# Three column tiles of a decoder layer's input projection computed side by side instead of one after the other

## The chip, the cores and the metric

The kernel runs on one core of one Trainium2 chip. The metric is device microseconds (us) of one execution, the median of several runs. TensorE (PE) multiplies, ScalarE (ACT), VectorE (DVE) and GpSimd (POOL) do the elementwise work, and SyncE (SP) issues every DMA from one queue, in the order of the program.

## The reference

One step of one decoder layer for 512 prompt tokens and 32 sample tokens (8 sequences with 4 new tokens each), all in float32:

```python
h = rms_norm(x, norm_pre)                    # over the 2048 model channels
z = jnp.einsum('btd,de->bte', h, w_in)       # 2048 x 7680: q, k, v, gates, conv inputs
att = attend(q, k, v)                        # 12 heads, three dilated windows; samples read a cache
u = c_a * jax.nn.sigmoid(c_b)                # conv branch: depthwise conv, LayerNorm, swish, pointwise
mix = jnp.concatenate([att * silu(g_att), c * silu(g_conv)], axis=-1)
y = jnp.einsum('bte,ed->btd', mix, w_out)    # 2048 x 2048
return x + rms_norm(y, norm_post), new_conv, new_kv
```

The updated cache (`new_kv`) is an output too: most of its bytes are a plain copy of the old cache.

## The kernel before

All 544 tokens lie along the free axis, and channels lie on the 128 partitions. x comes transposed, in 16 blocks of 128 channels (eight loads `xr0` to `xr7` of two blocks each, six buffers). The input projection has 60 column tiles of 128 columns, the output projection 16. The weights of a tile come in four quarters (`raw`, 128x512, 256 KB, six buffers); quarter m belongs to tile m // 4.

Products keep float32 accuracy by splitting both operands in two reduced-precision parts: x into `xh` (ACT, line 243) and `xl` (DVE, line 244), a weight quarter into `wh` (ACT, line 793) and `wl` (POOL, line 794). For each of the 16 blocks of rows and each half of the tokens (272) there are three matmuls: xh by wh, xl by wh, xh by wl. A tile is thus 16 x 2 x 3 = 96 matmuls, which accumulate in two PSUM banks, one for each half.

`split_x(c)` splits the two blocks of one x load. It also sums the squares of x for the RMS norm: ACT squares most blocks (`sq`, three buffers), DVE each fourth (line 250), and the sums of even blocks are added by POOL and those of odd blocks by DVE (`ssum`, line 254). The norm is a factor R for each token, applied when a product is taken out of PSUM by DVE (`evac`, or lines 879 to 882 for queries). `make_R` calls `token_rsqrt`: TensorE sums the squares over the partitions (`rqx`), ACT and DVE form the inverse root, DVE builds five diagonal matrices (line 201), TensorE spreads them over all partitions (`rbx`), and ACT copies them to R (line 295).

`project(n)` computes tile n. For the first tile it alternates: split two loads of x, split the next weight quarter, multiply. The first tile's product is taken out after `make_R`; the tiles behind it find all of x split. `split` looks two quarters ahead (`LOOK`) and loads five further (`AHEAD`). After each quarter comes `tick()`: it advances the side work (attention, conv, samples, the bias tables of `make_tabs`) by a step, and tops up the bulk copy:

```python
        bulk(START + PACE * pe[0])
```

`bulk` issues copies of old cache rows (1152 KB each) on SP's queue as long as the bytes sent stay below a budget: START bytes, and PACE bytes for each row passed through TensorE so far (`pe[0]`). So the DMA traffic that no one waits for is spread over the kernel. Each engine executes its instructions in the order in which the program gives them; `in_order` fixes that.

`make_tabs` is side work added after the first tile: two small products `tb` (line 279) with a copy by ACT each (line 280), then a memset and a small DVE product `lt` (lines 283, 284), and two products `rb` (line 289) with a copy by ACT each (line 290). All four use PSUM bank "s". From the fourth tile on, the samples' cache rows are loaded in units (`kvf`, `kvm`) and DVE computes their scores.

Of the kernel before, what the change touches and what calls it, by code (L numbers as in the profile page):

```python
# [18 lines left out]
P = 128  # L19
# [21 lines left out]

# ticks (quarters of a weight tile) for a batch's keys and for its values
UTK, UTV = 3.8, 3.7
# bytes in the DMA queue: at the start, and for each row that passes through the tensor engine
START, PACE = 8_000_000, 158.35

# [4 lines left out]
def backward(t, c0, c1):  # L51
    # columns c0..c1 of a 512-column tile, the last one first, counted from the end
    a = t[:, 0:1]
    return bass.AP(tensor=a.tensor, offset=a.offset + SEQ - 1 - c0, ap=[list(a.ap[0]), [-1, c1 - c0]])
# [28 lines left out]
def body(tc, xT, w_in, w_out, ckv, cconv, relb, vecs, pww, c_oht, c_ohr, c_lmr, c_tm, c_pick,  # L83
# [12 lines left out]

    # rows that the products given so far pass through the tensor engine
    pe = [0]
# [26 lines left out]

# [1 line left out]
    raws = {}  # L127
# [17 lines left out]
    def load_w(m):  # L145
        # a quarter of a tile: four of its 16 blocks of rows
        if m >= 4 * NTILE or m in raws:
            return
        n, qt = divmod(m, 4)
        raw = wpool.tile([P, 4, P], F32, tag="raw", name=f"raw{m}", bufs=6)  # L150
        dma(raw, w_in[order[n], qt] if n < N_IN else w_out[n - N_IN, KORD[4 * qt] // 4])
        raws[m] = raw
# [3 lines left out]

# [1 line left out]
    ident = keep.tile([P, P], F32, name="ident")  # L158
# [7 lines left out]
    dtab = dram.tile([NH, TW], F32, name="dtab")  # L166
    # rows 32g + 4h + t: biases of a group's heads for the new token t; rows 96..127: log counts of (b, t)
    base = keep.tile([P, RW], F32, name="base")
# [10 lines left out]

    def token_rsqrt(sums, pool, name):  # L180
        # (sum over the partitions / 2048 + EPS) ** -0.5 of each token, in all partitions: two halves in PSUM.
        # The tokens lie in the partitions for the root itself, with one Newton step after the table's root.
        ps = bank("q", f"rq{name}")
        for j, st in enumerate(STARTS):
# [9 lines left out]
        nc.vector.tensor_scalar(w, w, -0.5, 1.5, op0=ALU.mult, op1=ALU.add)  # L194
        nc.vector.tensor_tensor(r, r, w, op=ALU.mult)
        out = []
        for hf, (j0, j1) in enumerate(((0, 3), (2, 5))):
            ps = bank("st"[hf], f"rb{name}{hf}")
            for j in range(j0, j1):
                if hf == 0 or j > 2:  # L200
                    nc.vector.tensor_scalar(diag[:, j, :], ident, r[:, j:j + 1], 2048.0, op0=ALU.mult, op1=ALU.mult)
                t0, t1 = max(j * P, hf * HT), min(j * P + P, hf * HT + HT)
                d0 = t0 - STARTS[j]
                mm(ps[:, t0 - hf * HT:t1 - hf * HT], ones, diag[:, j, d0:d0 + t1 - t0], start=True, stop=True)
            out.append(ps)
        return out

    def rsqrt(dst, ps, w, scale, pool, tag="rs", bufs=2):
        # dst = (scale * ps + EPS) ** -0.5, one Newton step after the table's root
        s = pool.tile([P, HT], F32, tag=tag, name=f"rs{len(rs_n)}", bufs=bufs)  # L210
        rs_n.append(0)
        nc.scalar.activation(s[:, :w], ps, AF.Sqrt, bias=epsc[:, 0:1], scale=scale)
        yield
        nc.vector.reciprocal(dst, s[:, :w])
        nc.scalar.activation(s[:, :w], ps, AF.Identity, bias=epsc[:, 0:1], scale=scale)
        yield
        nc.vector.tensor_tensor(s[:, :w], s[:, :w], dst, op=ALU.mult)
        nc.vector.tensor_tensor(s[:, :w], s[:, :w], dst, op=ALU.mult)
        nc.vector.tensor_scalar(s[:, :w], s[:, :w], -0.5, 1.5, op0=ALU.mult, op1=ALU.add)
        nc.vector.tensor_tensor(dst, dst, s[:, :w], op=ALU.mult)  # L220
# [34 lines left out]

    # bias tables
    rel33 = ip.tile([33, NH], F32, name="rel33")
# [34 lines left out]

    def make_R():
        for hf, ps in enumerate(token_rsqrt(ssum, ip, "x")):
            nc.scalar.copy(R[:, hf * HT:hf * HT + HT], ps[:, :HT])

# [1 line left out]
    d2d = [(b, a0, s0) for b in range(NB) for a0 in range(0, 96, 16) for s0 in (0, 6)]  # L298
# [9 lines left out]

# [1 line left out]
    mixg = [keep.tile([P, 4, TOK], F32, name=f"mix{i}") for i in range(4)]  # L310
# [83 lines left out]

# [1 line left out]
    conv_u = {}  # L396

    def conv_in(ct, a, bt):
        # u = a * sigmoid(b), with sigmoid(b) = (1 + tanh(b / 2)) / 2
        ccv = state["ccv"]  # L400
# [36 lines left out]
    def conv_ln():  # L437
# [6 lines left out]
        pw = load_pw(1)  # L444
        # the ones matrix holds 1/2048, and a mean over 512 channels is 4 times that sum
        for hf in range(2):
# [23 lines left out]
        for ct in range(4):  # L470
# [5 lines left out]
            yield  # L476
        # the products of the later channels wait beside, those of the first replace their own operands
        res = [cc[:, 0, :]] + [apool.tile([P, TOK], F32, tag="up", name=f"pwo{i}", bufs=2) for i in range(2)]
# [21 lines left out]

# [1 line left out]
    sp_ = ExitStack()  # L502
# [43 lines left out]

    # the group's new k or v, one row per token
    def tm_mm(g, nm):
# [14 lines left out]
    def k_phase(g, before):  # L563
# [16 lines left out]
        def qr_copy(b):  # L580
            # column p gets the query of token p % 4
            if b < NB:
# [14 lines left out]
        def recent(b, ktn):  # L597
            # the last 128 rows of the cache: each batch's queries stand alone among zeros
            for hh in range(G4):
# [163 lines left out]

# [1 line left out]
    sides = []  # L765
# [31 lines left out]
    def project(n, hi, lo, out):  # L797
        # out(hf, z) takes a half's product over
        z = [None, None]

        def part(c, hf):
            wh, wl = splits[4 * n + c]
            sl = slice(hf * HT, hf * HT + HT)
            if z[hf] is None:
                # the second tile takes a bank more, while the first waits for its tokens' scale
                z[hf] = bank("att" if n == 1 and hf == 1 else "z", f"z{n}_{hf}")[:, :HT]
            for kk in range(4):
# [4 lines left out]

        for a in range(LOOK + 1 if n else 1):
            split(4 * n + a)
        for c in (0, 2):
            for hf in range(2):
                if n == 0:
                    split_x(2 * (c + hf))
                    split_x(2 * (c + hf) + 1)
                    split(4 * n + c + hf + 1)  # L820
                    part(c + hf, 0)
                    part(c + hf, 1)
                else:
                    split(4 * n + c + hf + LOOK)
                    part(c, hf)
                    part(c + 1, hf)
                if c + hf == 3:
# [3 lines left out]
        for c in range(4):  # L831
            splits[4 * n + c] = None


    def samples():
# [8 lines left out]

    load_w(0)
    for c in range(8):
        xrs[c] = load_x(c)
        if c % 2:
            load_w(1 + c // 2)
    bulk(START)  # L850
    load_tabs()
    for n in range(N_IN):
        c = order[n]
        kind, h = divmod(c, NH)
        if n == 3:
            ini.close()
# [14 lines left out]

        def out(hf, z):
            if n == 0 and hf == 0:
                make_R()
            if c >= NH:
                evac(z, t_, hf)
            elif hf == 0:
                # the prompt's queries in backward order: a row of biases then runs forward in the table
                nc.vector.tensor_tensor(backward(t_, 0, HT), z[0], R[:, :HT], op=ALU.mult)
# [3 lines left out]

        project(n, xh, xl, out)
        if n == 0:
            add(make_tabs(), 0, 0)
        if n == 1:
            load_toep(0)
        if n == 3:
            add(samples(), 0, 1)  # L890
# [43 lines left out]

# [1 line left out]
    op = ctx.enter_context(tc.tile_pool(name="outp", bufs=1))  # L936
# [14 lines left out]
    for i in range(16):  # L951
# [13 lines left out]
        if i == 14:  # L965
            # brings the root's table in before it is waited for
            nc.scalar.activation(root, epsc, AF.Sqrt)
    bulk(1 << 60)
    halves = token_rsqrt([ysum, ylast], op, "y")
    R2 = op.tile([P, TOK], F32, name="R2")  # L970
# [17 lines left out]

# [1 line left out]
def _tables():  # L990
# [36 lines left out]
    for t in range(NT):  # L1027
        tm[t, :, t] = 1.0
    # (h, b, t) from (h, t) in each group's rows, and from (b, t) in the last ones; then the rows of each group
    pick = np.zeros((4, 32, G4, NB, NT), np.float32)  # L1030
# [63 lines left out]
```

## Time and profile before

| what | value |
|---|---|
| median of 3 runs | 1206.57 us (1206.16 to 1207.15) |
| span of the profiled execution, first to last instruction | 1204.4 us |
| median less span | 2.2 us |
| TensorE busy in that span | 1146.9 us (95%) |
| DMA, share of 16 engines' time of the one queue | 93.0% |

The profiled execution's own time is not listed apart from its span; the 2.2 us are what lies around the span if it ran like the median. In the profile a merged row with "x2" gives the start of the first instruction and the busy time of both. TensorE's rows are given for each matmul: matmuls overlap, so the distance from one start to the next is the cost of one, not the duration.

### The profile page before, as it was taken

The page shows a single profiled execution, that of the slowest core. Times are in us where ns is not written, and L with a number is a line of the kernel's source. Part 1 is how long each engine was busy: PE and PEld are TensorE (multiplying, and loading weights), DVE is VectorE, ACT ScalarE, POOL GpSimd, SP SyncE. Part 2 cuts the span into 40 slices and gives each one's busy share as a digit, 9 for nine tenths or more (in the row PEclk, how much of TensorE's full clock was granted, in tenths as well). Part 3 has the DMA queues.
Part 4 walks back from the last instruction along what each step waited for, and adds up shares of the span by engine and source line. Part 5 has one row for each costly group of instructions (what it writes and reads, how often), then busy time and mean ns, then how long its engine had stood idle before and what let it go on. Part 6 is the DMA issues. An engine that isn't in the chain of part 4 may idle for free.

```text
span 1204.4 us, 25446 instructions
## 1 busy us (share of the span) xinstructions
PE 1146.9 (95%) x10014; PEld 1092.5 (91%) x10014; DVE 665.0 (55%) x1962; ACT 380.1 (32%) x761; POOL 457.3 (38%) x387
## 2 busy tenths in 40 slices
PE   4899999999999999999999999999999989999990
PEld 4799999999999999999999999999999979999990
DVE  7306989789889988777232676982221140000018
ACT  6223333322123332331343333322212243333320
POOL 5244333343333332343233222433433534444425
PEclk9799999999999999999999999999999989999995
DMA  9599999989999999999999999999989968999993
GB/s 338 214 372 331 335 369 339 337 274 325 318 343 346 341 344 345 376 356 324 361 330 337 361 350 325 326 311 377 332 310 344 336 225 342 355 348 337 355 332 150
DMA packets 158572, 396.55 MB, mean 329 GB/s; under 512 B 19623, under 2 KB 22439, under 8 KB 155252
## 3 DMA queue, kind: packets, MB, share of 16 engines
q1 hardware_dynamic: 158452, 394.93, 93.0%
q8 instruction: 78, 1.28, 0.4%
q14 instruction: 42, 0.34, 0.1%
HBM read 295.46 MB, written 212.66 MB: 422 GB/s over the span
## 4 chain that ended last, share of the span: by engine, by line
PE 54%; DVE 3%; issue 2%; POOL 1%; DMA 1%; ACT 0%; SPq 0%; POOLq 0%; ACTq 0%
PE z L104 45%; PE o L106 3%; PE pwp L104 1%; DVE y L980 1%; PE s L104 1%; PE att L104 1%; DVE y L981 1%; POOL wl L794 1%; DMA kvf<-in_ckv_dram 1%; PE t L110 1%; DVE qsc L624 0%; PE pm L104 0%; PE pvar L104 0%; PE kt L110 0%; PE sn L106 0%
## 5 line engine op out<-in xcount | busy, mean ns | idle before, releaser
L794 POOL TENSOR_TENSOR wl<-raw,wh 128x512 fp32r<-128x512 f32 x304 | 412.6, 1367 | 586.0 <-ACT wh L793 536.9
L104 PE MATMUL z<-xh,wh 128*128 128x272 f32 x1920 | 575.5, 300 | 7.4 <-ACT xh L243 7.4
L104 PE MATMUL z<-xl,wh 128*128 128x272 f32 x1920 | 557.2, 290 | 9.7 <-DVE xl L244 9.5
L104 PE MATMUL z<-xh,wl 128*128 128x272 f32 x1920 | 556.8, 290 | 0.0
L104 PEld LDWEIGHTS z<-xh,wh 128*128 128x128 f32 x1920 | 365.8, 191 | 23.2 <-issue 11.8
L104 PEld LDWEIGHTS z<-xl,wh 128*128 128x128 f32 x1920 | 365.2, 190 | 14.3 <-DVE xl L244 12.3
L104 PEld LDWEIGHTS z<-xh,wl 128*128 128x128 f32 x1920 | 365.4, 190 | 0.0
L793 ACT CAST wh<-raw 128x512 fp32r<-128x512 f32 x304 | 184.8, 618 | 248.8 <-PE z L104 130.4
L104 PE MATMUL z<-mh,wl 128*128 128x272 f32 x512 | 149.1, 291 | 2.4 <-POOL wl L794 2.4
L104 PE MATMUL z<-mh,wh 128*128 128x272 f32 x512 | 148.9, 291 | 1.8 <-ACT mh L943 1.8
L104 PE MATMUL z<-ml,wh 128*128 128x272 f32 x512 | 148.7, 291 | 1.6 <-DVE ml L944 1.6
L315 DVE TENSOR_TENSOR t<-z,R 128x272 f32<-128x272 f32 x96 | 42.0, 438 | 183.9 <-PE z L104 172.5
L624 DVE SCALAR_TENSOR_TENSOR qsc<-kvf,qb 128x128 f32<-128x128 f32 x288 | 125.8, 437 | 8.8
L624 DVE SCALAR_TENSOR_TENSOR qsc<-kvm,qb 128x128 f32<-128x128 f32 x288 | 112.5, 391 | 8.7
L960 DVE TENSOR_TENSOR ysum<-ysum,ysq 128x272 f32<-128x272 f32 x28 | 12.4, 443 | 166.0 <-ACT ysq L959 166.0
L423 DVE SCALAR_TENSOR_TENSOR mix<-up,vec,mix 128x512 f32<-128x512 f32 x120 | 104.0, 867 | 0.0
L104 PEld LDWEIGHTS z<-mh,wl 128*128 128x128 f32 x512 | 97.7, 191 | 2.6 <-POOL wl L794 2.6
L104 PEld LDWEIGHTS z<-mh,wh 128*128 128x128 f32 x512 | 98.0, 192 | 2.0 <-ACT mh L943 2.0
L104 PEld LDWEIGHTS z<-ml,wh 128*128 128x128 f32 x512 | 97.6, 191 | 2.1 <-DVE ml L944 2.0
L425 DVE SCALAR_TENSOR_TENSOR mix<-us,vec,mix 128x32 f32<-128x32 f32 x120 | 59.8, 499 | 0.0
L344 ACT ACTIVATE pr<-pr,nm 128x128 f32<-128x128 f32 (+3 forms) x48 | 27.1, 564 | 81.0 <-DVE nm L343 80.2
L954 ACT ACTIVATE y<-z,vec 128x272 f32<-128x272 f32 x32 | 15.6, 488 | 82.6 <-PE z L104 82.6
(181 smaller groups left out, 952.2 us busy)
## 6 DMA issues: line engine op xcount, KB each, us to landing
out_dram<-in_ckv_dram SPq DMA_DIRECT2D x96, 1152.0 KB, 8.3
raw<-in_w_in_dram SPq DMA_DIRECT2D x240, 256.0 KB, 6.1
kvm<-in_ckv_dram SPq DMA_DIRECT2D x48, 1024.0 KB, 8.8
out_dram<-kvm SPq DMA_DIRECT2D x48, 1024.0 KB, 10.5
kvf<-in_ckv_dram SPq DMA_DIRECT2D x144, 256.0 KB, 8.6
out_dram<-kvf SPq DMA_DIRECT2D x96, 256.0 KB, 4.6
raw<-in_w_out_dram SPq DMA_DIRECT2D x64, 256.0 KB, 6.2
out_dram<-kvf SPq DMA_DIRECT2D x48, 128.0 KB, 7.7
```

Of the source, the lines that this page charges most:

```text
L104: nc.tensor.matmul(out, lhsT, rhs, start=start, stop=stop)
L106: nc.tensor.matmul(out, lhsT, rhs, start=start, stop=stop, tile_position=tile_position)
L110: nc.tensor.transpose(out, in_, eye)
L315: nc.vector.tensor_tensor(dst[:, sl], z[hf][:, :HT], R[:, sl], op=ALU.mult)
L344: nc.scalar.activation(pr[:, :w], pr[:, :w], AF.Exp, bias=nm[:, 0:1], scale=1.0, accum_out=nm[:, 1:2])
L423: nc.vector.scalar_tensor_tensor(cc[:, ct, :SEQ], up[:, j:j + SEQ], wj, cc[:, ct, :SEQ], op0=ALU.mult, op1=ALU.add)
L425: nc.vector.scalar_tensor_tensor(cs, us[:, :, j:j + NT], wj, cs, op0=ALU.mult, op1=ALU.add)
L624: nc.vector.scalar_tensor_tensor(scr, src[:, hh * P:hh * P + P], SCALE, qb[:, hh * P:hh * P + P], op0=ALU.mult, op1=ALU.mult, accum_out=sd ...
L793: nc.scalar.copy(wh, raw)
L794: nc.gpsimd.tensor_tensor(wl, raw, wh.bitcast(F32), op=ALU.subtract)
L954: nc.scalar.activation(yt[i // 4][:, i % 4, sl], z[hf], AF.Copy, scale=V(V_GPOST, i))
L960: nc.vector.tensor_tensor(ysum[:, sl], ysum[:, sl], sq, op=ALU.add)
```

## The change

The first three tiles (`NF`) are no longer computed by `project`. A new function, `project_first`, holds six PSUM banks (three tiles, two halves) and goes through x block by block: for each of the 16 blocks it issues the 18 matmuls of all three tiles. The weight quarters of the three tiles are split together, three for each four blocks of x, one step ahead; the odd steps' `wh` and `wl` borrow buffers that attention uses later. The loads of weights and x are issued in the order of their use. `make_R` is called behind the first block of the last step: `token_rsqrt` issues the sums, the root and the diagonals, then calls `between`, which issues the matmuls of the last three blocks, and then spreads R. Only then are all six halves taken out, and the bias tables are made in four ticks one after the other, before the fourth tile starts. START goes from 8,000,000 to 14,000,000 bytes, PACE from 158.35 to 156.0. Removed comments are not shown.

```diff
-START, PACE = 8_000_000, 158.35
+START, PACE = 14_000_000, 156.0
+NF = 3
...
-    def token_rsqrt(sums, pool, name):
-        ps = bank("q", f"rq{name}")
+    def token_rsqrt(sums, pool, name, between=None):
+        ps = bank("t", f"rq{name}")
...
+        for j in range(5):
+            nc.vector.tensor_scalar(diag[:, j, :], ident, r[:, j:j + 1], 2048.0, op0=ALU.mult, op1=ALU.mult)
+        if between:
+            between()
...
-                if hf == 0 or j > 2:
-                    nc.vector.tensor_scalar(diag[:, j, :], ident, r[:, j:j + 1], 2048.0, op0=ALU.mult, op1=ALU.mult)
...
-    def make_R():
-        for hf, ps in enumerate(token_rsqrt(ssum, ip, "x")):
+    def make_R(between):
+        for hf, ps in enumerate(token_rsqrt(ssum, ip, "x", between)):
...
+    def project_first(outs):
+        tags = (("z", "z"), ("z", "att"), ("q", "acc"))
+        z = [[bank(tags[n][hf], f"z{n}_{hf}")[:, :HT] for hf in range(2)] for n in range(NF)]
+        spare = ((("pt", 2), ("pt", 2), ("vtm", 1)), (("pr3", 1), ("pw", 1), ("toep", 1)))
+        def split_first(c):
+            out = []
+            for n in range(NF):
+                raw = raws.pop(4 * n + c)
+                raws[4 * n + c] = None
+                if c % 2:
+                    wh, wl = [apool.tile([P, 4, P], F32R, tag=spare[i][n][0], name=f"w{'hl'[i]}{4 * n + c}",
+                                         bufs=spare[i][n][1]) for i in range(2)]
+                else:
+                    wh, wl = [wpool.tile([P, 4, P], F32R, tag=f"w{x}", name=f"w{x}{4 * n + c}", bufs=4)
+                              for x in "hl"]
+                nc.scalar.copy(wh, raw)
+                nc.gpsimd.tensor_tensor(wl, raw, wh.bitcast(F32), op=ALU.subtract)
+                out.append((wh, wl))
+            return out
+        def rows(c, ws, k0, k1):
+            for k in range(4 * c + k0, 4 * c + k1):
+                for n in range(NF):
+                    wh, wl = [w[:, k % 4, :] for w in ws[n]]
+                    for hf in range(2):
+                        sl = slice(hf * HT, hf * HT + HT)
+                        mm(z[n][hf], wh, xh[k][:, sl], start=(k == 0), stop=False)
+                        mm(z[n][hf], wh, xl[k][:, sl], start=False, stop=False)
+                        mm(z[n][hf], wl, xh[k][:, sl], start=False, stop=(k == KT - 1))
+        split_x(0)
+        ws = split_first(0)
+        split_x(1)
+        for c in range(4):
+            if c < 3:
+                nxt = None
+                split_x(2 * c + 2)
+                nxt = split_first(c + 1)
+                split_x(2 * c + 3)
+                rows(c, ws, 0, 4)
+                ws = nxt
+                for a in range(2 * c, 2 * c + 2):
+                    load_w(4 * NF + a)
+                now[0] += 4
+                bulk(START + PACE * pe[0])
+            else:
+                rows(c, ws, 0, 1)
+                make_R(lambda: rows(c, ws, 1, 4))
+        for n in range(NF):
+            for hf in range(2):
+                outs[n](hf, z[n])
...
-    load_w(0)
-    for c in range(8):
-        xrs[c] = load_x(c)
-        if c % 2:
-            load_w(1 + c // 2)
+    for c in range(4):
+        load_w(c)
+        xrs[2 * c] = load_x(2 * c)
+        load_w(4 + c)
+        xrs[2 * c + 1] = load_x(2 * c + 1)
+        load_w(8 + c)
     bulk(START)
     load_tabs()
...
-        project(n, xh, xl, out)
-        if n == 0:
-            add(make_tabs(), 0, 0)
-        if n == 1:
-            load_toep(0)
+        if n < NF:
+            first.append(out)
+            if n == NF - 1:
+                project_first(first)
+                add(make_tabs(), 0, 0)
+                for _ in range(4):
+                    tick()
+                load_toep(0)
+        else:
+            project(n, xh, xl, out)
```

`project` loses its branches for the first two tiles; for the others it issues what it did.

## Rows read from the trace of the kernel before

**Rows 1.** The page, 40 equal slices, in tenths (granted clock of TensorE; DMA).
```profile
PEclk9799999999999999999999999999999989999995
DMA  9599999989999999999999999999989968999993
```

**Rows 2.** Stretches: length; busy PE, PEld, DVE, ACT, POOL; granted clock; DMA share; GB/s.
```profile
20.00:30.00 10.00, 5.84 (x27) 5.40 (x27) 9.96 (x10) 5.05 (x9) 7.24 (x4) 0.98 0.93 314
30.00:40.00 10.00, 8.21 (x45) 7.68 (x45) 8.10 (x9) 3.64 (x5) 3.50 (x2) 0.68 0.73 282
40.00:50.00 10.00, 8.22 (x45) 8.14 (x45) 2.95 (x14) 2.07 (x5) 2.52 (x2) 0.67 0.05 5
...
400.00:700.00 300.00, 299.27 (x2687) 279.55 (x2686) 194.46 (x652) 102.71 (x218) 98.43 (x92) 1.00 0.99 346
```

**Rows 3.** TensorE's waits in the first 60 us: total, times, longest.
```profile
PE z L104 <- DVE xl L244: 9.5, 7, 3.3
```

**Rows 4.** Timeline of DVE, 0 to 62 us: start, busy, line, operation.
```profile
7.35 0.78 DVE L244 SCALAR_TENSOR_TENSOR xl<-xr,vec,xh 128x544 fp32r<-128x544 f32 x1 [6.21 <-ACT xh L243]
...
9.87 3.58 DVE L244 SCALAR_TENSOR_TENSOR xl<-xr,vec,xh 128x544 fp32r<-128x544 f32 x2
...
26.99 3.58 DVE L244 SCALAR_TENSOR_TENSOR xl<-xr,vec,xh 128x544 fp32r<-128x544 f32 x2
...
31.12 1.47 DVE L244 SCALAR_TENSOR_TENSOR xl<-xr,vec,xh 128x544 fp32r<-128x544 f32 x2
...
36.03 1.47 DVE L244 SCALAR_TENSOR_TENSOR xl<-xr,vec,xh 128x544 fp32r<-128x544 f32 x2
37.43 0.71 DVE L254 TENSOR_TENSOR ssum<-ssum,sq 128x544 f32<-128x544 f32 x1
```

**Rows 5.** Timeline of POOL, 0 to 62 us.
```profile
26.45 1.75 POOL L794 TENSOR_TENSOR wl<-raw,wh 128x512 fp32r<-128x512 f32 x1
...
47.26 2.52 POOL L794 TENSOR_TENSOR wl<-raw,wh 128x512 fp32r<-128x512 f32 x2 [11.73 <-ACT wh L793]
```

**Rows 6.** Timeline of ACT, 41 to 62 us.
```profile
46.28 0.39 ACT L295 COPY R<-rbx 128x272 f32<-128x272 f32 x1 [0.92 <-PE rbx L104]
46.56 1.14 ACT L793 CAST wh<-raw 128x512 fp32r<-128x512 f32 x2
52.12 0.57 ACT L280 COPY tabs<-tb 12x512 f32<-12x512 f32 x1 [4.42 <-PE tb L104]
...
57.22 0.58 ACT L290 COPY base<-rb 96x512 f32<-96x512 f32 x1 [3.27 <-PE rb L104]
```

**Rows 7.** Timeline of TensorE, 38 to 61 us.
```profile
39.41 2.29 PE L104 MATMUL rqx<-ones,ssum 128*128 128x1 f32 x20
43.47 2.77 PE L104 MATMUL rbx<-diagx,ones 128*128 128x128 f32 x12 [1.78 <-DVE diagx L201]
46.05 0.57 PE L104 MATMUL z<-xh,wh 128*128 128x272 f32 x1
...
50.05 0.33 PE L104 MATMUL z<-xh,wl 128*128 128x272 f32 x1
...
51.06 1.02 PE L104 MATMUL tb<-oht,rel 33*12 33x512 f32 x2
52.75 0.39 PE L104 MATMUL tb<-oht,rel 33*12 33x128 f32 x2 [0.66 <-ACT tabs L280]
```

**Rows 8.** Timeline of DVE, 60 to 77 us: second halves of tiles two and three leave.
```profile
63.93 0.41 DVE L881 TENSOR_TENSOR mix<-z,R 128x240 f32<-128x240 f32 x1 [3.25 <-PE z L104]
64.25 0.18 DVE L882 TENSOR_TENSOR sq<-z,R 128x32 f32<-128x32 f32 x1
...
75.95 0.41 DVE L881 TENSOR_TENSOR mix<-z,R 128x240 f32<-128x240 f32 x1 [2.55 <-PE z L104]
```

**Rows 9.** The tile kvm: its loads, and their times from issue to landing.
```profile
L95 SPq DMA_DIRECT2D kvm<-in_ckv_dram x48: 378/385/1590, 73.4 to 910.9; - x48
...
DMA to landing us min/median/max: 6.8/9.7/13.3
```

More of the change, by code (lines that the diff above doesn't have):

```diff
@@ L804, in part @@
             if z[hf] is None:
-                z[hf] = bank("att" if n == 1 and hf == 1 else "z", f"z{n}_{hf}")[:, :HT]
+                z[hf] = bank("z", f"z{n}_{hf}")[:, :HT]
             for kk in range(4):
@@ L811, in part @@
                 mm(z[hf], wl[:, kk, :], hi[k][:, sl], start=False, stop=(k == KT - 1))
-        for a in range(LOOK + 1 if n else 1):
+        for a in range(LOOK + 1):
             split(4 * n + a)
@@ L816, in project @@
             for hf in range(2):
-                if n == 0:
[L818 to L826, printed above, removed]
+                split(4 * n + c + hf + LOOK)
+                part(c, hf)
+                part(c + 1, hf)
                 if c + hf == 3:
@@ L843, in samples @@
             state["vdone"] = g
-    load_w(0)
-    for c in range(8):
-        xrs[c] = load_x(c)
-        if c % 2:
-            load_w(1 + c // 2)
+    for c in range(4):
[4 more added lines that the diff above has]
+        load_w(8 + c)
     bulk(START)
     load_tabs()
+    first = []
     for n in range(N_IN):
@@ L854, in body @@
         kind, h = divmod(c, NH)
-        if n == 3:
+        if n == NF:
             ini.close()
@@ L870, in body, with out @@
             t_ = apool.tile([P, TOK], F32, tag=nm, name=f"t{n}", bufs=2 if nm == "k" else 1)
-        def out(hf, z):
-            if n == 0 and hf == 0:
-                make_R()
+        def out(hf, z, t_=t_, c=c, g=g if c < 3 * NH else None, hh=hh if c < 3 * NH else None, nm=nm):
             if c >= NH:
@@ L882, in out @@
                 nc.vector.tensor_tensor(smp[g][nm][:, hh, :], z[1][:, SEQ - HT:], R[:, SEQ:], op=ALU.mult)
-        project(n, xh, xl, out)
-        if n == 0:
-            add(make_tabs(), 0, 0)
-        if n == 1:
-            load_toep(0)
-        if n == 3:
+        if n < NF:
[8 more added lines that the diff above has]
+            project(n, xh, xl, out)
+        if n == NF:
             add(samples(), 0, 1)
```

## The prediction

> **What bounds the kernel now.** First the page's strip of 40 slices [rows 1]: the granted clock is at its top but for the second slice, one near the end and the last, and DMA is at its top too, but for the second slice and the last fifth. With TensorE busy for 95% of the span, the kernel is a full engine beside a nearly full DMA queue, and what either can gain lies at the edges. The stretches [rows 2] say it closer: from 400 to 700 us TensorE is busy for 299.27 of 300 us and DMA for 0.99. At the front it is otherwise. From 20 to 30 us TensorE is busy for 5.84 us, while DVE is busy for 9.96: splitting x fills DVE, and the first tile has only six matmuls for each block of x. From 30 to 50 us the granted clock is 0.68 and 0.67, and from 40 to 50 us DMA stands nearly still (0.05). The waits name the release: TensorE waits 9.5 us for `xl` in seven places [rows 3]. Last I read the timelines of the front, engine by engine [rows 4 to 8].
>
> The place to compare is the start of the fourth tile, from where both kernels do the same work. Before, the third tile's second half leaves at 75.95 us [rows 8], so TensorE starts the fourth tile at about 75.8. The second tile's leaves at 63.93: 12.02 us for 96 matmuls, 0.125 us for each at full clock.
>
> **The cost of a POOL instruction to DVE.** Two `xl` alone take 1.47 us, 0.735 each; beside POOL's work two take 3.58, 1.79 each [rows 4]. A `wl` alone is 1.26 (two in 2.52), beside DVE 1.75 [rows 5]. So DVE and POOL go in pairs of about 1.8 us, and each POOL instruction costs DVE 1.79 - 0.735 = 1.05 us. The change puts 12 `wl` instead of 4 into the stretch in which x is split.
>
> The page "SBUF — State Buffer" of the Trainium skill, section "Who interferes with whom", says that a DVE instruction with two inputs in SBUF and a GpSimd instruction that reads SBUF exclude each other for their whole length. By that alone each `wl` would cost DVE 1.26, and the gain below would be 1.7 us smaller; the pairs of the trace (1.8, not 0.735 + 1.26 = 2.0) agree with the exclusion, but less sharply.
>
> **The change, step by step.**
>
> *Loads.* The first weight quarter and the first x load stand at the head of the queue as before, so the first `xl` starts at 7.35 again [rows 4]. Ahead of the rest now lie twelve weight quarters (0.262 MB each) among eight x loads (0.557 MB): with the vectors 7.7 MB by the shapes. The six buffers for raw quarters make SP wait for POOL from the seventh on. The later x loads then come some 10 us later, but still before ACT asks for them; I cost this at nothing. The cover is ACT's and DVE's own backlog; without it a late x load shifts everything behind it by its delay, 2 us for 2.
>
> *Splitting x.* Before, from the first `xl` (7.35) to the end of the last (36.03 + 1.47 = 37.50) it is 30.15 us, with four `wl` inside. Now there are eight more: 8 x 1.05 = 8.4 us. Three casts (0.57 each, 1.7 us [rows 6]) stand on ACT between the first x load and the second; the third `xl` started at 9.87 before and can now start when ACT gets there, about 1.1 us later. Last `xl` ends: 37.50 + 8.4 + 1.1 = 47.0; with the last sum (0.71 [rows 4]) 47.7. Bounds on the 8.4: nothing if TensorE, not DVE, is the slower one (next step), and 8 x 1.75 = 14.0 if POOL's whole contended length is added.
>
> *The matmuls of three tiles.* Each block of x now feeds 18, 2.25 us at full clock. x comes at (47.0 - 7.35) / 16 = 2.5 us per block: TensorE follows closely, nearly full, and I take the clock to rise as it did before, after a cold stretch. That stretch is in the rows: from 46.05 to 50.05, 18 matmuls in 4.0 us, 0.222 each, the 1.2 GHz level [rows 7]. The first block of weights is whole only when POOL has split three quarters: ACT, behind two splits and a square, casts the first by about 9.2, and three times 1.75 makes 14.5 us. From there TensorE alone would need 15.5 blocks x 2.25 = 34.9 plus 2 us for the cold start: 51.4, about the end of a schedule that DVE sets too. So neither has much slack.
>
> *The norm.* The sums now stand behind the 13th block. TensorE waits for them until 47.7, then: sums 2.29, the last three blocks 54 x 0.125 = 6.75, spreading 2.77 [rows 7]: 59.5. The root and the diagonals, on which TensorE waited before (39.41 + 2.29 = 41.70 to 43.47), are hidden under the 54 matmuls: 1.8 us saved, within this sum. In the output's norm the same edit only moves the diagonals ahead of products that wait for the first of them anyway: nothing.
>
> *From there to the fourth tile.* What ran among matmuls now stands alone. After R's second copy (0.39) DVE takes out the five halves left: some 0.5 us each (0.41 + 0.18 where it is in two parts [rows 8]), 2.7 us, then `lt`, near +3.3 us. TensorE's first table products (1.02 and 0.39) end before that. The third product (as long as the first, 1.02) runs to 4.4, its copy on ACT (0.58) to 5.0, the fourth product to 5.9, its copy to 6.4. Only then is the fourth tile's first quarter cast (0.57, to 7.0), and POOL's `wl` (1.26) ends at 8.3 [rows 5 to 7]. Two matmuls go ahead of it (0.25). So the fourth tile runs as if from 59.5 + 8.3 - 0.25 = 67.6. In half-idle 8 us the clock should fall, as it did around 43 us: 18 matmuls in 4.0 us instead of 32, 1.8 us. Sum: 69.4, against 75.8: 6.4 us gained. Bounds of this step: 4.7 (no loss of clock, the copies half hidden) to 11.
>
> *START and PACE.* The budget is 6.0 MB larger at the start, less 2.35 bytes for each row: some 78,000 rows by the fourth tile, 0.2 MB. DMA's idle time from 30 to 50 us (0.27 + 0.95 of 10 us [rows 2], 12 us, at 346 GB/s 4.2 MB) is filled with it. TensorE's lead adds 6.4 us x 345 GB/s = 2.2 MB of demand. The queue is then longer by 6.0 - 0.2 + 2.2 - 4.2 = 3.8 MB, 11 us. A cache load takes 9.7 us (13.3 at most) and there is a unit each (910.9 - 73.4) / 47 = 17.8 us [rows 9], one unit ahead. So most is hidden by that lead; raw weights have six buffers of 3 us each. I take 0, with 0 to 11 as bounds.
>
> The total: the profile's span of 1204.4 less 6.4 is 1198.0; with the 2.2 around it, 1200.2. That 2.2 is the whole difference between the span and the median of the runs shown.
>
> **The rivals.**
>
> *TensorE sets the front, and DMA's filled hole counts.* Three full tiles end at 51.4, then sums and spreading (5.1): 56.5; fourth tile at +8.1 and no cold start: 64.6, gain 11.2: 1195.4. For it: DVE's extra 8.4 us then hide, and DMA, as full as TensorE, gains 12 us at the same place. Against: DVE is busy for 9.96 of 10 us and gets more to wait for.
>
> *DVE and POOL cost more than pairs.* 14.0 instead of 8.4, and the clock cold for the last blocks behind a longer wait for the sums (54 x 0.097 = 5.2 at most, half taken): 8.2 us later, 1208.4, which is no change that can be told. For it: POOL also gets three `wl` at a time, and the square buffers, three of them, chain ACT, DVE and POOL. Against: 1.79 was measured beside both kinds of POOL work.
>
> *Slower: the longer queue.* 3.8 MB more ahead of the cache loads: 9.7 + 11 = 20.7 us against a lead of 17.8, so DVE's scores wait, the matmuls' banks are not emptied, and TensorE stands. It decides where landing passes 17.8 us; the price is the whole excess if it must be worked off in waits, 11 us: 1200.2 + 11 = 1211. For it: DMA at 0.99 from 400 to 700 us. Against: the excess shrinks by PACE, and SP stands while a buffer is full, which lets the queue drain.
>
> *It does not do what it says.* TensorE, waiting for each block, stays at 1.2 GHz: 288 x 0.222 = 64 us from 10 us on: 74 + 5 + 8.3 = 87, 11 us late: 1218. Against: the clock rose after 4.0 us of unbroken matmuls [rows 7], and the work per block is tripled.
>
> **How the numbers follow.** Forecast 0.52 (1197 to 1204), TensorE-set 0.20, DVE and POOL dear 0.14, longer queue 0.10, cold 0.04. The range from 1193 to 1208 takes in the first rival with a further 2.4 us below it, and above the forecast half of the two costly cases; it leaves out the cold case and the rest of those. A difference under 0.2% (2.4 us) cannot be told here. Faster: 0.49 of the forecast's, 0.20 and 0.03 of the queue's, where little of it is paid: 0.72. Same: 0.03 of the forecast's, 0.09 of the second rival's and 0.02 of the queue's: 0.14. Slower: 0.05 of each of the last two of these and 0.04: 0.14.
>
> **What would show it.** After: last `xl` near 47; `rqx` near 48; `rbx` ending near 60; the fourth tile's first matmuls near 67, with a stretch of 0.22 us steps; DMA near its top from 25 to 60 us; a kvm landing median above 9.7 in the first 200 us. It is wrong if the last `xl` comes before 43 or after 52, if TensorE runs at 0.22 steps between 25 and 45 us, or if waits for kvf or kvm appear behind 100 us.

## The result, and the profile after

The changed kernel takes 1215.61 us (median of 11 runs, 1213.3 to 1218.84) against 1207.15 for the kernel before beside it: ratio 1.0068, 95% interval [1.0052, 1.0085], so about 8 us slower. The forecast was 1200.2, the range ended at 1208. The direction is that of the third rival, the longer queue, which had 1211.

First the page's strip of 40 slices, as in [rows 1].

```profile
PEclk9887999999999999999999999999999989999995
DMA  8989999999999999999998999989999859999983
```

The front of the kernel is better filled than before, but the granted clock is now low in the second to fourth slice (30 to 121 us), not in the second alone. The stretches, with the columns of [rows 2]:

```profile
20.00:30.00 10.00, 10.00 (x82) 10.00 (x82) 9.97 (x7) 4.03 (x7) 9.92 (x7) 1.00 0.93 321
30.00:40.00 10.00, 9.76 (x77) 9.40 (x76) 9.96 (x8) 6.46 (x12) 7.82 (x6) 1.00 1.02 354
40.00:50.00 10.00, 6.13 (x38) 5.60 (x37) 7.63 (x7) 2.03 (x3) 5.17 (x4) 0.77 0.89 282
50.00:60.00 10.00, 10.00 (x62) 10.00 (x62) 2.00 (x11) 0.27 (x1) 0.00 (x0) 0.72 0.87 314
...
90.00:100.00 10.00, 0.84 (x7) 0.63 (x6) 0.00 (x0) 0.00 (x0) 0.00 (x0) 0.65 0.86 279
100.00:110.00 10.00, 6.96 (x41) 6.64 (x42) 0.44 (x1) 4.09 (x8) 5.21 (x5) 0.66 1.07 422
```

From 20 to 40 us TensorE is now busy for 19.76 of 20 us at full clock; it was 14.05. The loss stands further down: from 90 to 100 us TensorE works for 0.84 us, ACT, DVE and POOL not at all, and from 100 to 110 the granted clock is 0.66. The waits of TensorE from 60 to 130 us (total, times, longest) name it:

```profile
PE z L106 <- ACT wh L797: 12.8, 2, 11.7
```

and the timeline shows where, in the fifth tile:

```profile
102.51 0.59 PE L106 MATMUL z<-xh,wh 128*128 128x272 f32 x1 [11.67 <-ACT wh L797]
```

ACT had waited too, for a raw quarter of weights (22.45 us, until 101.84). So the question goes to SP, whose timeline of the stretch is:

```profile
50.77 0.84 SPq L97 DMA_DIRECT2D raw<-in_w_in_dram  x2
51.66 0.58 SPq L97 DMA_DIRECT2D out_dram<-in_ckv_dram  x1
52.34 1.01 SPq L97 DMA_DIRECT2D raw<-in_w_in_dram  x2
53.40 2.39 SPq L97 DMA_DIRECT2D out_dram<-in_ckv_dram  x2
55.88 1.17 SPq L97 DMA_DIRECT2D raw<-in_w_in_dram  x2
57.11 9.98 SPq L97 DMA_DIRECT2D out_dram<-in_ckv_dram  x6
67.44 0.33 SPq L97 DMA_DIRECT2D dtab<-tabs  x1
89.67 0.33 SPq L97 DMA_DIRECT2D toep<-dtab  x1
90.10 1.92 SPq L97 DMA_DIRECT2D kvf<-in_ckv_dram  x3
92.06 0.59 SPq L97 DMA_DIRECT2D kvm<-in_ckv_dram  x1
92.76 3.61 SPq L97 DMA_DIRECT2D raw<-in_w_in_dram  x5
```

Read it from the bottom. The next weights go out at 92.76. Ahead of them SP stood from 67.8 to 89.67, because `toep` is read from `dtab`, and the 30 KB of `dtab`, stored at 67.44, landed only then. Ahead of `dtab` nine bulk copies of 1.18 MB went out within 16 us. The six quarters issued from 50.77 to 57.05 are all that TensorE had: four for the fourth tile, two for the fifth, and it ran out of them at 90.8. SP's waits from 60 to 95 us say the same in one row, and the next row, of the DMA issues from 60 to 90 us, gives the copies' median time to landing:

```profile
SPq L97 <- DMA dtab<-tabs: 21.8, 1, 21.8
```

```profile
out_dram<-in_ckv_dram SPq DMA_DIRECT2D x4, 1152.0 KB, 22.0
```

Placed beside the trace of before product by product, the changed kernel is 3.1 us ahead when the fourth tile's second half leaves, and 11.2 us behind when the fifth tile's does (in each fence first the fourth tile, then the fifth; first fence of before, second of after). From there it stays 10.8 to 11.3 us behind until 967 us of before. All of the loss, some 14 us, lies between 85 and 108 us.

```profile
87.98 0.41 DVE L881 TENSOR_TENSOR mix<-z,R 128x240 f32<-128x240 f32 x1 [2.55 <-PE z L104]
...
100.45 0.44 DVE L315 TENSOR_TENSOR t<-z,R 128x272 f32<-128x272 f32 x1 [2.99 <-PE z L104]
```

```profile
84.87 0.41 DVE L932 TENSOR_TENSOR mix<-z,R 128x240 f32<-128x240 f32 x1 [2.55 <-PE z L106]
...
111.67 0.44 DVE L319 TENSOR_TENSOR t<-z,R 128x272 f32<-128x272 f32 x1 [3.04 <-PE z L106]
```

### The profile page after: what moved, and what is told of

It is laid out like the page before. It is cut to its first block, busy times and chain, and to the rows that moved or that the text cites. A ratio compares the mean times of both kernels' runs of the same rounds, so it can differ in the third digit from the quotient of the medians.

```text
span 1213.8 us, 25447 instructions
## 1 busy us (share of the span) xinstructions
PE 1146.0 (94%) x10014; PEld 1090.6 (90%) x10014; DVE 672.7 (55%) x1962; ACT 379.0 (31%) x761; POOL 459.9 (38%) x387
## 4 chain that ended last, share of the span: by engine, by line
PE 52%; DVE 5%; issue 2%; POOL 1%; ACT 0%; DMA 0%; SPq 0%; POOLq 0%; ACTq 0%
PE z L106 43%; PE o L108 3%; DVE qsc L628 2%; PE pwp L106 1%; DVE y L1037 1%; PE s L106 1%; PE att L106 1%; DVE y L1038 1%; POOL wl L798 1%; PE t L112 1%; PE pvar L106 0%; PE pm L106 0%; DVE mix L971 0%; DMA out_dram<-kvf 0%; PE rby L106 0%
## 5 line engine op out<-in xcount | busy, mean ns | idle before, releaser
L798 POOL TENSOR_TENSOR wl<-raw,wh 128x512 fp32r<-128x512 f32 x292 | 394.9, 1363 | 592.7 <-ACT wh L797 537.2
L797 ACT CAST wh<-raw 128x512 fp32r<-128x512 f32 x292 | 177.0, 618 | 253.6 <-PE z L106 126.9
## 6 DMA issues: line engine op xcount, KB each, us to landing
out_dram<-kvm SPq DMA_DIRECT2D x48, 1024.0 KB, 10.3
```

The source lines that it names most:

```text
L797: nc.scalar.copy(wh, raw)
L798: nc.gpsimd.tensor_tensor(wl, raw, wh.bitcast(F32), op=ALU.subtract)
```

## The experiments

Two theories stood after this. **The dependence**: `load_toep(0)`, now called right behind the tables, makes SP wait where it may not. **The budget**: START and PACE put too many bulk copies ahead of `dtab` and of the weights. Times are medians; each ratio is to the kernel before, run beside it.

**1. toep_later.** The call that makes SP wait is put two tiles later.

```diff
                 for _ in range(4):
                     tick()
-                load_toep(0)
         else:
             project(n, xh, xl, out)
+        if n == NF + 1:
+            load_toep(0)
```

> The changed kernel with one line moved: the first load of the bias rows from the dtab table (toep) is issued behind the fifth tile instead of ahead of the fourth. START and PACE stay at the new values. Theory 1, SP's order: SP stands 21.8 us behind toep for the store of dtab, and the weights behind it come late; with toep later TensorE's wait of 11.7 us near 90 us goes, with the cold clock behind it some 14 us, and the time falls from 1215.6 to about 1202. Theory 2, the queue itself: the store took 21.8 us because six bulk copies lay ahead of it, and weights issued from 69 us on lie behind the same copies and land at 91 to 97 us; TensorE still waits 2 to 8 us there, and the time is 1205 to 1211.

Measured: 1216.05, ratio 1.0071 [1.0049, 1.0092]: nothing changed. SP's timeline shows why:

```profile
68.46 0.33 SPq L97 DMA_DIRECT2D dtab<-tabs  x1
89.41 1.92 SPq L97 DMA_DIRECT2D kvf<-in_ckv_dram  x3
```

The wait moved to the next DMA that depends on that store: the profile puts 20.5 us before `kvf` down to `dtab<-tabs`, since `kvf` is laid into memory that `tabs` held. The experiment took away one of two such dependences and so could not decide.

**2. old_budget.** The changed kernel with the constants of before.

```diff
-START, PACE = 14_000_000, 156.0
+START, PACE = 8_000_000, 158.35
```

> The changed kernel with the old START and PACE (8,000,000 and 158.35), all else as changed. Theory 1: the store of dtab finds a short queue, SP's wait for it falls from 21.8 to 5 to 9 us, TensorE's wait near 90 us goes, and the time is about 1202 to 1204. Theory 2 gives the same time here, from the short queue alone; what it cannot have is a wait of SP that stays near 20 us while TensorE doesn't wait. If both fall, the side-by-side part alone is worth minus 3 to minus 5 us against the kernel before.

Measured: 1201.5, ratio 0.9956 [0.9939, 0.9972]. Side by side alone is a gain of 3.4 to 7.4 us, where the forecast was 6.4; the budget costs 1215.6 - 1201.5 = 14 us. Its stretches from 30 to 50 us, with the columns of [rows 2], and then SP's timeline:

```profile
30.00:40.00 10.00, 10.00 (x83) 10.00 (x82) 9.96 (x8) 6.45 (x12) 7.82 (x6) 1.00 0.77 254
40.00:50.00 10.00, 6.18 (x39) 5.66 (x38) 7.39 (x7) 1.77 (x2) 4.93 (x4) 0.86 0.96 358
```

```profile
49.12 3.31 SPq L97 DMA_DIRECT2D out_dram<-in_ckv_dram  x2
64.63 0.33 SPq L97 DMA_DIRECT2D dtab<-tabs  x1
72.62 0.33 SPq L97 DMA_DIRECT2D toep<-dtab  x1
...
76.25 3.81 SPq L97 DMA_DIRECT2D raw<-in_w_in_dram  x5
```

Nothing is issued between the copies of 49.12 and `dtab`; SP then stands for 7.6 us instead of 21.8, and the weights go out at 76.25 instead of 92.76. TensorE's 11.7 us wait is gone. The first fence holds the point that the prediction missed: with the old budget DMA is idle for 2.7 us from 30 to 50 us, where it was idle for 12 before [rows 2]. Side by side fills the hole by itself: `bulk` adds PACE for each row that the program has *given* to TensorE, and `project_first` gives the rows of three tiles in three steps, with only six weight quarters between the copies. By 52 us 10 copies are out; before it was 5. The six megabytes of START come on top: 15 copies ahead of `dtab` instead of 10.

**3. before_new_budget.** The kernel before, with START and PACE of after (the same two constants, the other way round).

> The kernel before with the new START and PACE (14,000,000 and 156.0) and nothing else changed. Theory 1: dtab is stored at 53 us, toep asked for at 61 us; six quarters of weights are in the buffers, and the queue is not yet full when the store goes, so SP's wait is some 10 us at most and TensorE's is under 2: the time stays within 2 us of 1207. Theory 2: the budget alone makes the early loads late, with the same bulk bytes ahead of the weights: TensorE waits 5 us or more between 40 and 110 us, and the time is 1211 or more.

Measured: 1207.61, ratio 1.0004 [0.9987, 1.002]: nothing. There the copies leave one at a tick between weights, and the seven early ones of 13.78 us work on into the idle stretch: from 40 to 50 us the DMA share is 0.83, where it was 0.05 [rows 2]. Of SP's waits from 60 to 95 us, the one for `dtab`:

```profile
SPq L95 <- DMA dtab<-tabs: 1.8, 1, 1.8
```

So the budget is harmful only together with the other half of the change.

**4. both.** Experiments 1 and 2 together.

> Both edits on the changed kernel: toep behind the fifth tile, and the old START and PACE. Theory 1: nothing left to gain over either edit alone, 1201 to 1203. Theory 2: the same as the old budget alone, within 1 us of it. If this one is faster than the old budget alone by more than 2 us, SP's wait costs even with a short queue; if it is slower than toep moved alone, the larger START is a gain once SP does not stand.

Measured: 1201.47, ratio 0.9958 [0.9939, 0.9978], the same as the old budget alone. The place of `load_toep` matters in neither.

**5. sp_free.** New budget, `toep` later, and the table held in two attention tiles, so that neither `toep` nor `kvf` waits for the store.

```diff
-            nc.scalar.copy(tabs[:, c0:c0 + w], ps[0:NH, :w])
-        dma_late(dtab, tabs, 2)
+            tb = apool.tile([P, 4, P], F32, tag="vtm", name="tb1") if c0 else apool.tile([P, SEQ], F32, tag="pt",
+                                                                                          name="tb0", bufs=2)
+            tb = tb[0:NH, 0, :] if c0 else tb[0:NH, :]
+            nc.scalar.copy(tb, ps[0:NH, :w])
+            dma_late(dtab[:, c0:c0 + w], tb, 2)
```

> Moving toep alone changed nothing, because the cache load behind it (kvf) takes memory in which the table tile (tabs) lay, and so waits for the same store of dtab: SP stood 20.5 us at kvf. Here neither waits: toep behind the fifth tile, and the table in two tiles of the attention pool, stored in two parts. START and PACE stay new, and the store still goes behind the same bulk copies. Theory 1, SP's order: SP doesn't stand near 68 us, weights are issued from 69 us on, TensorE's wait near 90 us is under 2 us: about 1202. Theory 2, the length of the queue: those weights lie behind the same six copies, land at 91 to 97 us, and TensorE waits 2 to 8 us: 1205 to 1211.

Measured: 1211.57, ratio 1.004 [1.0027, 1.0053]. Beside experiment 1, by their ratios, this is 0.3% or some 4 us better; the two intervals overlap by a little. SP's timeline and, of its waits from 60 to 95 us, the first:

```profile
68.50 0.96 SPq L97 DMA_DIRECT2D dtab<-tb  x2
72.66 7.92 SPq L97 DMA_DIRECT2D kvf<-in_ckv_dram  x3
...
87.23 5.76 SPq L97 DMA_DIRECT2D raw<-in_w_in_dram  x5
```

```profile
SPq L97 <- DMA out_dram<-in_ckv_dram: 24.8, 9, 3.2
```

The dependence is gone and SP stands all the same, now in nine pieces and for the copies themselves: the three `kvf` take 7.92 us to issue. The weights go out at 87.23, still 11 us later than with the old budget, and TensorE waits 7.3 us for them. In the profile the lead over before falls from 3.8 us at the fourth tile to 6.5 us behind at the fifth: 10.3 us, where the changed kernel loses 14.3. So the dependence has a part of the 14 us, about 4, and the copies ahead of it have the rest, about 10; by the times alone, whose intervals overlap, the 4 would not be shown.

**6. gap_filled.** Old budget; to see whether the 8 us gap behind the norm can be closed, the tables are made inside the three tiles (two banks) and the fourth tile's first quarters are split ahead of the norm.

```diff
+                if c == 2:
+                    next(tabs_)
...
+                next(tabs_)
+                for a in range(LOOK + 1):
+                    split(4 * NF + a)
                 rows(c, ws, 0, 1)
                 make_R(lambda: rows(c, ws, 1, 4))
```

> Old budget. The bias tables are made inside the three tiles (first products ahead of the third step, the others behind it, in two banks), dtab is stored there, and the fourth tile's first three weight quarters are split before the norm. Theory: after R is spread, TensorE stood for tables and splits from 61.5 to 69 us and then ran cold for 4 to 8 us; with that filled the fourth tile starts near 62 us, and the time is 1194 to 1197, against 1201.5 with the old budget alone. Rival: the tables only move (their 3.3 us and ACT's and DVE's waits come back in the third step, where x is late), and the time stays at 1199 to 1202.

Measured: 1201.62, ratio 0.9963 [0.9946, 0.998]: no better than experiment 2. The gap did close. Its fourth tile's second half leaves at 76.89, a lead of 11 over before; the lead stays between 8 and 11.2 us, is 11.2 again at 321 us of before, and 5.4 from 332 us of before on. The timeline of TensorE shows where it starts to go:

```profile
320.54 1.63 PE L108 MATMUL o<-kvm,spt 128*32 128x128 f32 x32 [3.62 <-DMA kvm<-in_ckv_dram]
```

A lead at the front is a demand on DMA that runs 11 us earlier all the way; that DMA, near its top, does not follow is what this one wait suggests, and experiments 7 and 12 bear on it.

**7. sums_later.** Experiment 6 with the norm's sums behind two blocks of x instead of one, and ACT's table loaded ahead of the first x.

```diff
+    nc.scalar.copy(R[:, 0:1], epsc)
...
-                rows(c, ws, 0, 1)
-                make_R(lambda: rows(c, ws, 1, 4))
+                rows(c, ws, 0, 2)
+                make_R(lambda: rows(c, ws, 2, 4))
```

> As the last one, and the norm's sums stand behind two blocks of the last step instead of one, and an early copy on ACT brings the table load (1.28 us) ahead of the first x. Theory: TensorE waited 3.9 us for the sums from 43.8 to 47.7 us and ran them cold (4.0 instead of 2.3 us); with a block more ahead of them that wait falls by 2 us, the cold by 1 to 2, the start by 0.8: 1 to 4 us less than the run before, 1191 to 1195. Rival: the sums set the end by DVE's chain anyway, and only the 0.8 us are won.

Measured: 1196.39, ratio 0.9918 [0.9897, 0.9939], with a wide spread (1193.8 to 1202.96). Two things changed at once, so the gain isn't shared out between them. In the profiled run, the slowest of them, a lead of 10 us falls to 3 between 475 and 490 us of before: TensorE is busy for 6.30 of the 10 us from 480 to 490, with the clock at 0.83 and DMA at 1.02, and at 485.45 DVE has waited 5.95 us for a store (`out_dram<-t`) to land; before it waited 0.19 at that place.

**8. sums_later_new_budget.** Experiment 7 with START and PACE of after.

> As the last one with the new START and PACE. dtab is stored near 35 us here, so SP need not stand for it at 68. Theory 1: the larger START costs nothing then, within 2 us of the run with the old budget. Theory 2: the weights of the tiles from the fourth on come late behind the longer queue, TensorE waits 4 us or more between 60 and 110 us: 4 to 10 us slower than with the old budget.

Measured: 1208.35, ratio 1.0012 [1.0001, 1.0024]: 12 us worse than experiment 7. Here `dtab` is stored at 49.87 and no wait for it shows, but SP stands for 46.5 us in 16 pieces behind the copies. Of SP's timeline one line, and of its waits from 40 to 110 us the first:

```profile
49.87 0.65 SPq L97 DMA_DIRECT2D dtab<-tabs  x1
```

```profile
SPq L97 <- DMA out_dram<-in_ckv_dram: 46.5, 16, 4.0
```

So the budget costs without the dependence and without the gap of tables and splits. The cost comes by late weights here too, in two places. ACT waits 6.9 and 6.7 us for the fourth tile's quarters, whose splits now stand ahead of the root, so TensorE waits 6.4 us for the diagonals; at the fourth tile that leaves a lead of 10.5 us instead of 12.9. At the sixth tile, between 90 and 109 us, another 8.6 us go: TensorE waits there for `wh` (3.0 us) and `wl`, and the granted clock is 0.69 from 90 to 100 us.

**9. six_first.** The changed kernel with 14 MB for the first call of `bulk` alone, and the old constants for the top-ups behind it. Are the first six copies at fault (23.9 us, they delay the loads behind them), or the nine later ones?

```diff
-START, PACE = 14_000_000, 156.0
+START, PACE = 8_000_000, 158.35
...
-    bulk(START)
+    bulk(14_000_000)
```

> The changed kernel with the larger budget only in the first call: six bulk copies go behind the first loads as in the changed kernel (bulk up to 14,000,000 bytes, once), all later calls use START 8,000,000 and PACE 158.35, so one copy instead of nine is issued between the third step and the store of dtab. Theory A: what makes the weights late are the later copies (52 to 67 us), which lie ahead of the store of dtab, the cache loads and the weights; without them the queue is short by 68 us: 1200 to 1203, as with the old budget or a little better. Theory B: the six first copies do it, by putting off the tables' inputs and the fourth tile's weights to 50 us: 1207 or more.

Measured: 1201.6, ratio 0.9965 [0.9954, 0.9976]. SP's timeline:

```profile
53.72 2.49 SPq L97 DMA_DIRECT2D out_dram<-in_ckv_dram  x4
64.61 0.33 SPq L97 DMA_DIRECT2D dtab<-tabs  x1
71.85 0.32 SPq L97 DMA_DIRECT2D toep<-dtab  x1
```

The six early copies go out at 23.84, as in the changed kernel, and alone they cost nothing. With four later ones instead of nine the loss is gone, so it takes the five more top-ups. Ahead of `dtab` lie ten copies, as in experiment 2; whether nine top-ups would do harm without the six early copies, no run shows.

**10 to 12.** From here to a better version: experiment 7 with six copies first (10), with a slower PACE (11), and with both (12).

> The best version so far (tables and splits inside the three tiles, sums behind two blocks, early table load, old budget; 1196.4) with six copies in the first call instead of one or two, as in the run before this. Theory A: DMA's idle time at the front is used, the lead of 11 us over the kernel before is given back later or not at all: 1192 to 1196. Theory B: late weights or tables at the front, 1200 or more. Third way: no difference, 1195 to 1198, if the lead is lost to the order of DMAs in the middle of the kernel and not to their sum.

> The best version so far with START 8,000,000 and PACE 156.0 instead of 158.35: 6 MB less bulk before the end, 3 MB less by the middle, five more copies left over at TensorE's end. Theory: the lead of 11 us is lost where DMA runs full (in the profiled run at 455 to 490 us, where SP stood 13 us for a store of kvm); with less bulk by then it keeps more of it: 1190 to 1195. Rival: that loss is a chance meeting of DMAs and not of their sum: 1194 to 1199, and the five copies left over show in the tail.

> Both: six copies in the first call, and PACE 156.0 with START 8,000,000 behind it. If both edits work for the same reason (DMA's slack), about as the better of the two or 1 to 2 us below, 1190 to 1194; if the six copies make the front late, 1198 or more.

Measured: 1194.6, 0.9906 [0.9893, 0.9919]; 1193.93, 0.9911 [0.9895, 0.9926]; 1192.09, 0.988 [0.9865, 0.9894]. The first two can't be told from experiment 7; the interval of the third lies just below that of experiment 7 and touches that of experiment 10, and it is faster than both kernels. That a slower PACE leaves DMA room later on, and the six copies first make up for the bytes, is how I read it; no run shows it by itself. Of experiment 12, the stretch from 25 to 50 us with the columns of [rows 2], and the fourth tile's second half on DVE:

```profile
25.00:50.00 25.00, 25.00 (x184) 23.08 (x183) 21.32 (x17) 10.62 (x19) 15.95 (x11) 0.97 0.91 295
```

```profile
69.82 0.41 DVE L939 TENSOR_TENSOR mix<-z,R 128x240 f32<-128x240 f32 x1 [2.55 <-PE z L106]
```

TensorE does not stop from 25 to 50 us, and the lead over before at the fourth tile is 18.2 us, of which the end keeps 13.

## Why the prediction was wrong

**Splitting x: right.** Forecast: last `xl` ends at 47.0, the sum at 47.7. DVE's timeline of after:

```profile
38.60 3.56 DVE L248 SCALAR_TENSOR_TENSOR xl<-xr,vec,xh 128x544 fp32r<-128x544 f32 x2
...
45.56 1.47 DVE L248 SCALAR_TENSOR_TENSOR xl<-xr,vec,xh 128x544 fp32r<-128x544 f32 x2
46.95 0.71 DVE L258 TENSOR_TENSOR ssum<-ssum,sq 128x544 f32<-128x544 f32 x1
```

It ends at 47.03 and 47.66. The pairs hold: three `wl` of POOL in a row take 5.24 us beside DVE, 1.75 each as in [rows 5], and two `xl` 3.56. The exclusion that "SBUF — State Buffer" of the Trainium skill states (section "Who interferes with whom") agrees in kind; as a sum of the two lone durations it would, by the prediction's estimate, have put this end 1.7 us later. Part of the hit is luck: the first `xl` started at 8.14, not 7.35, because ACT's table load now waits for x (it ran at 6.06; before, at 0.73, under the wait for the first weights). That I had at nothing; from there to the end it took 38.9 us, 0.8 less than the forecast's 39.65.

**TensorE beside it: right.** It ran at full clock from 20 to 40 us, so the cold rival did not come true, nor, since it waited 2.2 us for the last sum, the TensorE-set one.

**The norm and the tables: 2 us too cheap.** TensorE's timeline, against [rows 7]:

```profile
47.72 4.00 PE L106 MATMUL rqx<-ones,ssum 128*128 128x1 f32 x18 [2.18 <-DVE ssum L258]
51.58 0.57 PE L106 MATMUL z<-xh,wh 128*128 128x272 f32 x1
...
60.19 1.42 PE L106 MATMUL rbx<-diagx,ones 128*128 128x128 f32 x12
61.53 1.02 PE L106 MATMUL tb<-oht,rel 33*12 33x512 f32 x2
...
70.20 0.59 PE L106 MATMUL z<-xh,wl 128*128 128x272 f32 x1 [0.53 <-POOL wl L798]
...
76.03 0.29 PE L106 MATMUL z<-xh,wh 128*128 128x272 f32 x1
```

The sums took 3.9 us instead of 2.29 and the 54 matmuls 8.6 instead of 6.75, since the clock fell in the wait for the sums (0.77 granted from 40 to 50 us, 0.72 from 50 to 60); the spreading took 1.3 instead of 2.77. That makes 61.5 instead of 59.5. From there to the first `wl` product it is 8.7 us, forecast 8.3. The cold steps then lasted to 76.03, some 7 us with one break of 0.5 instead of the 4 of [rows 7]: 1 us more. Together 3.4 us of the 6.4, which leaves the 3.1 measured at the fourth tile. With the old budget it is 4.2 (83.74), and the medians of experiment 2 give 5.6, with an interval (3.4 to 7.4) that holds the forecast's 6.4. So the mechanism of the side-by-side part was right and its sum a little high.

**START and PACE: the step that failed.** "I take 0, with 0 to 11 as bounds" measured 14. Three things in it were wrong. The hole was counted as free for START, while the other half of the change had filled it (12 us before, 2.7 in experiment 2); without it the same sum gives not 3.8 but 3.8 + 9.3 x 0.346 = 7.0 MB, 20 us, above the bound of 11. The excess was then set against the cache units' lead and not against what else stood in SP's queue: the store of `dtab`, on which the next load depends, and behind it the weights, of which six buffers give TensorE 18 us at full clock, while SP did not issue a quarter for 36 us (57.05 to 92.76). And "SP stands while a buffer is full, which lets the queue drain" was held against the rival: but the next load that needs a buffer came up at 92.76, behind all the copies, so no full buffer could hold these back.

**Rival 3: right in sign, not in place, and near in size by luck.** Its 11 us came from the sum that counted the hole as free. It looked for a late `kvm`. Here is the tile's summary for the first 200 us, before and after:

```profile
DMA to landing us min/median/max: 7.6/9.9/12.1
```

```profile
DMA to landing us min/median/max: 9.5/10.5/11.5
```

The median is above 9.7, as the forecast's sign asked, but it rose by only 0.6 us and is far from the 17.8 at which the rival would decide; over the whole run it is 9.2, below the 9.7 of [rows 9]. Among TensorE's waits from 60 to 130 us is none for `kvf` or `kvm`. The wait was SP's, ahead of the issue, where time from issue to landing does not see it.

## What to carry to other kernels

A budget of bytes that is driven by work *given* changes its meaning when work is given earlier: after such a change, list what each queue issues, in order, up to the first load that the critical engine needs, and set the bytes ahead of that load against the buffers it has. An idle stretch of DMA can be spent once. A lead won at the front of a kernel whose DMA is near its top may not hold: here 11 us became 5 (experiment 6) and 10 became 3 (the slowest run of experiment 7), each at a wait for a transfer to land.

## What the runs showed of the hardware

- A store of 30 KB took as long as the copies ahead of it: issued at 67.44, it let the next load go at 89.67, where the 1.18 MB copies around it took 22.0 us to land. "DMA: Bandwidth & Descriptors" of the Trainium skill (section "Queues, rings and completion order") says that descriptors are consumed in ring order on each DMA engine; the trace agrees, as far as landing times (22.2 us beside 22.0) can show it.
- SP itself stands while copies are outstanding that share no tile with the loads behind them: 24.8 us in nine pieces from 60 to 95 us in experiment 5, 46.5 us in 16 pieces from 40 to 110 us in experiment 8. I had thought of issuing as free. What exactly SP waits for, the traces don't show.
- The stretch of matmuls at the 1.2 GHz level (0.22 to 0.23 us from start to start) behind a half-idle time differs: 4.0 us in [rows 7], 5.8 without a break (70.20 to 76.03) behind the half-idle 8 us of the changed kernel, 3.4 (71.17 to 74.54) at the same place in experiment 2. What sets the length stays open.
